# A recurrent mixer on one core: 64-row products alternate between row halves, and four stages of it are staged anew

## Chip, core and metric

One core of a Trainium2 chip runs one program with two model blocks, one after the other. The metric is device time in microseconds (us), the median over runs. The program uses TensorE (PE) for matrix products and transposes, VectorE (DVE) and ScalarE (ACT) for elementwise work, GpSimd (POOL) for little, and SyncE (SP) for issuing weight transfers.

## The reference

The change touches one function only, the recurrent mixer of the second block's last layer, on S = 256 tokens, width D = 1024 and 16 heads of N = 64:

```python
def rwkv7_mixer(h, ...):
    xx = jnp.pad(h, ((0, 0), (1, 0), (0, 0)))[:, :-1] - h
    xr, xw, xk, xv, xa, xg = [h + xx * mu[i] for i in range(6)]
    r = xr @ w_r; k = xk @ w_k; v = xv @ w_v
    w_log = -softplus(-(w0 + tanh(xw @ w_dec1) @ w_dec2)) - 0.5
    a = sigmoid(a0 + (xa @ w_a1) @ w_a2)
    g = sigmoid(xg @ w_g1) @ w_g2
    kk = l2norm_per_head(k * k_k)
    k = k * (1.0 + (a - 1.0) * k_a)
    decay = exp(-exp(w_log))
    def step(state, ...):                       # per head, 64 x 64
        sa = state @ (-kk_t)
        state = state * w_t + sa * (kk_t * a_t) + v_t * k_t
        return state, state @ r_t
    y = per_head_norm(scan(step)) * lnx_g + lnx_b
    bonus = sum(r * k * r_k) * v
    return ((y + bonus) * g) @ w_o
```

## The kernel before, in words

Function `rwkv` computes this in float32. Features lie on the partitions, 128 at a time in KC = 8 chunks of 256 tokens; a chunk holds two heads, the upper one on partitions 0 to 63 and the lower one on 64 to 127. A product of 128 rows uses all partitions, a product of one head uses a row half of 64. A float32 product is two instructions on TensorE in the trace; where operands are split into a high and a low part of type fp32r, a product is three instructions of half the passes (`mm3`, lines 180 to 182), and the splitting costs ScalarE (L168, L275) and VectorE (L169, L276) an instruction each per piece.

The stages, with their places in microseconds from the start of the profiled span:

- **Stage A, 1938.4 to 2027.1.** Low-rank products `lora` (L1597) on the mixes `xw` and `xa`; the second half of k (`lin_raw`, L1585); the head lengths (`lengths`, L1685 to L1700); the low-rank pair's second factors, decay and a, with 64 rows each (`second`, L1614, first all of decay, then g's first factor, then all of a); the running sum L (L1653) and its exponentials Pi, Pv (L1665, L1666); r from raw float32 weights; `sources` and `kappa` (L1707 to L1718), which build the scaled keys be, ka and AR; the blocks `alpha` (L1838, 64 rows each, evacuated by L1844), from which `cut` (L1860) copies the diagonal 32 x 32 blocks; `rho` (L1723, L1724); the bonus (L1791, L1792).
- **The inverse, 2027.1 to 2058.4.** `invert32` runs 62 small steps on VectorE (L296 to L304) in a chain. TensorE meanwhile makes v (L1768), and ScalarE evacuates each half of it with 16 instructions per 128 tokens (L1754, L1756).
- **Stage B, 2058.4 to 2143.1.** The steps `inverse` for four pairs of (group of 4 heads, chunk of 128 tokens), with the rest as filler: blocks rho (L1838, masked on VectorE by L1842), `tokmajor` (L1804), `gates` (L1783); then `inverse` for the other four with `finish` of groups 0 and 1. `finish` is, for each of two token chunks tb: `pair_blocks` (L1820, 64 rows, 256 columns, masked by L1822), R (L1960 in the first chunk; L1967 with 128 rows and L1968 with 64 rows in the second), U (L1976), the state S0, and the output (L1995 and L1996; L2004 to L2006). Then come the head norm on VectorE (L2011 to L2014) and a transpose and split.
- **Stage C, 2143.1 to 2155.3**, the norm of groups 0 and 1; **stage D, 2155.3 to 2191.2**, `finish` of groups 2 and 3 with the first products of w_o. After that w_o goes on.

Work is written as generators. `weave(chains, filler, n)` takes a step from each chain and n from the filler after each; `part(gen, n)` takes n steps. The framework then orders each engine's instructions by the place in that text and by what is ready in its own model, so the order on an engine is fixed before the run. Waits between engines are semaphores. Small products go to banks of PSUM from a ring (`bank1`), and a bank is free again when its evacuation is done. `wraw` issues a weight transfer of 1 MB on SP's queue into a ring of buffers.

## Time and profile before

| | us |
|---|---|
| runs of the kernel before | 2420.02, 2418.22, 2420.16 (median 2420.02) |
| profiled execution | 2412.75, of it the span 2411.0 |
| PE busy in the span | 2350.1 (97%) |
| DVE, ACT, POOL busy | 1547.2 (64%), 1139.9 (47%), 90.2 (4%) |
| mean granted PE clock | 0.986 of full speed |

The profiled execution stands 0.3% under the median of the runs. "Busy" says that an engine has an instruction in flight, not that it is at its peak. A TensorE instruction's own duration is longer than the distance to the next one, because they are pipelined; where an instruction's cost is wanted, the distance between starts is what counts. The granted clock tells how much of TensorE's full rate was allowed in a stretch. Tile names such as ts, tp and mm are tags of PSUM banks; 64*128 in a row is rows by columns of the array used, so 64*128 is a product that uses one row half.

### The profile page before, as it was taken

The page shows a single profiled execution, that of the slowest core. Times are in us where ns is not written, and L with a number is a line of the kernel's source. Part 1 is how long each engine was busy: PE and PEld are TensorE (multiplying, and loading weights), DVE is VectorE, ACT ScalarE, POOL GpSimd, SP SyncE. Part 2 cuts the span into 40 slices and gives each one's busy share as a digit, 9 for nine tenths or more (in the row PEclk, how much of TensorE's full clock was granted, in tenths as well). Part 3 has the DMA queues.
Part 4 walks back from the last instruction along what each step waited for, and adds up shares of the span by engine and source line. Part 5 has one row for each costly group of instructions (what it writes and reads, how often), then busy time and mean ns, then how long its engine had stood idle before and what let it go on. Part 6 is the DMA issues. An engine that isn't in the chain of part 4 may idle for free.

```text
span 2411.0 us, 37594 instructions
## 1 busy us (share of the span) xinstructions
PE 2350.1 (97%) x15300; PEld 2090.5 (87%) x15300; DVE 1547.2 (64%) x2857; ACT 1139.9 (47%) x1912; POOL 90.2 (4%) x92
## 2 busy tenths in 40 slices
PE   9999999999999999999999999999999899989998
PEld 8878979899999988888799898899899776777997
DVE  6787558977788755555665576655655546536554
ACT  6556554135444444444644454544544324424443
POOL 0100002000000000000100001000000000110000
PEclk9999999999999999999999999999999989989999
DMA  4335443454444455555555542555555423102544
GB/s 175 136 123 178 158 157 123 140 177 172 160 161 172 165 195 195 195 202 192 181 178 177 211 147 98 180 178 192 184 176 191 154 79 114 53 18 97 193 175 157
DMA packets 55326, 380.15 MB, mean 158 GB/s; under 512 B 6384, under 2 KB 8048, under 8 KB 10352
## 3 DMA queue, kind: packets, MB, share of 16 engines
q1 hardware_dynamic: 55152, 377.75, 44.6%
q8 instruction: 120, 1.97, 0.3%
q14 instruction: 54, 0.44, 0.1%
HBM read 376.67 MB, written 1.05 MB: 157 GB/s over the span
## 4 chain that ended last, share of the span: by engine, by line
PE 86%; DVE 9%; ACT 2%; DMA 1%; issue 1%; POOL 1%; DVEq 0%; SPq 0%; ACTq 0%; POOLq 0%
PE acc L180 14%; PE acc L182 14%; PE acc L181 14%; PE mm L180 9%; PE mm L182 9%; PE mm L181 8%; PE mm L1585 2%; PE mm L989 2%; DVE wlo L169 1%; PE acc L1019 1%; PE mm L1575 1%; PE mm L1768 1%; ACT whi L168 0%; PE tp L245 0%; DVE H L901 0%
## 5 line engine op out<-in xcount | busy, mean ns | idle before, releaser
L169 DVE TENSOR_TENSOR wlo<-raw,whi 128x1024 fp32r<-128x1024 f32 (+1 forms) x768 | 758.2, 1000 | 450.5 <-ACT whi L168 449.1
L168 ACT ACTIVATE whi<-raw 128x1024 fp32r<-128x1024 f32 (+1 forms) x776 | 662.1, 872 | 730.9 <-PE acc L181 231.9
L180 PE MATMUL mm<-xhi,whi 128*128 128x256 f32 (+1 forms) x1368 | 395.7, 290 | 0.7 <-ACT xhi L250 0.6
L182 PE MATMUL mm<-xhi,wlo 128*128 128x256 f32 (+1 forms) x1368 | 388.6, 284 | 2.0 <-DVE wlo L169 2.0
L181 PE MATMUL mm<-xlo,whi 128*128 128x256 f32 (+1 forms) x1368 | 388.1, 284 | 0.0
L180 PE MATMUL acc<-xhi,whi 128*128 128x256 f32 x1280 | 362.5, 283 | 0.0
L182 PE MATMUL acc<-xhi,wlo 128*128 128x256 f32 x1280 | 362.2, 283 | 0.0
L181 PE MATMUL acc<-xlo,whi 128*128 128x256 f32 x1280 | 362.2, 283 | 0.0
L182 PEld LDWEIGHTS mm<-xhi,wlo 128*128 128x128 f32 (+1 forms) x1368 | 261.8, 191 | 4.1 <-DVE wlo L169 3.3
L180 PEld LDWEIGHTS mm<-xhi,whi 128*128 128x128 f32 (+1 forms) x1368 | 261.6, 191 | 3.6 <-issue 1.7
L181 PEld LDWEIGHTS mm<-xlo,whi 128*128 128x128 f32 (+1 forms) x1368 | 262.1, 192 | 0.6 <-DVE xlo L251 0.2
L181 PEld LDWEIGHTS acc<-xlo,whi 128*128 128x128 f32 x1280 | 245.7, 192 | 0.2
L180 PEld LDWEIGHTS acc<-xhi,whi 128*128 128x128 f32 x1280 | 245.7, 192 | 0.2
L182 PEld LDWEIGHTS acc<-xhi,wlo 128*128 128x128 f32 x1280 | 245.7, 192 | 0.0
L180 PE MATMUL acc<-whi,acts 128*128 128x512 f32 x424 | 164.9, 389 | 0.0
L181 PE MATMUL acc<-wlo,acts 128*128 128x512 f32 x424 | 164.9, 389 | 0.0
L182 PE MATMUL acc<-whi,acts 128*128 128x512 f32 x424 | 164.9, 389 | 0.0
L180 PE MATMUL acc<-whi,fhi 128*128 128x512 f32 x272 | 106.2, 391 | 0.1
L182 PE MATMUL acc<-whi,flo 128*128 128x512 f32 x272 | 105.9, 389 | 0.0
L181 PE MATMUL acc<-wlo,fhi 128*128 128x512 f32 x272 | 105.9, 389 | 0.0
L181 PEld LDWEIGHTS acc<-wlo,acts 128*128 128x128 f32 x424 | 79.6, 188 | 16.7
L182 PEld LDWEIGHTS acc<-whi,acts 128*128 128x128 f32 x424 | 79.6, 188 | 16.5
(767 smaller groups left out, 3817.2 us busy)
## 6 DMA issues: line engine op xcount, KB each, us to landing
raw<-in_l_ffn_gf_dram SPq DMA_DIRECT2D x80, 1024.0 KB, 4.8
raw<-in_peer_u_dram SPq DMA_DIRECT2D x64, 1024.0 KB, 4.9
raw<-in_peer_v_dram SPq DMA_DIRECT2D x64, 1024.0 KB, 4.9
raw<-in_l_ffn_wd_dram SPq DMA_DIRECT2D x44, 1024.0 KB, 4.7
raw<-in_w_gate_dram SPq DMA_DIRECT2D x8, 1024.0 KB, 4.9
raw<-in_w_pq_dram SPq DMA_DIRECT2D x8, 1024.0 KB, 4.9
raw<-in_l_ffn_gu_dram SPq DMA_DIRECT2D x8, 1024.0 KB, 4.8
raw<-in_w_mix_out_dram SPq DMA_DIRECT2D x4, 1024.0 KB, 4.9
```

Source lines behind the costliest of these rows:

```text
L168: nc.scalar.activation(out=hi[:, c:c + step], in_=raw[:, o + c:o + c + step], func=AF.Copy)
L169: eng.tensor_sub(lo[:, c:c + step], raw[:, o + c:o + c + step], hi[:, c:c + step].bitcast(F32))
L180: mm(out, lhsT=l[0], rhs=r[0], start=start, stop=False)
L181: mm(out, lhsT=l[0], rhs=r[1], start=False, stop=False)
L182: mm(out, lhsT=l[1], rhs=r[0], start=False, stop=stop)
L989: mm(o, lhsT=get[:, c:c + P], rhs=xn[:, kc, :], start=kc == 0, stop=kc == 7)
L1019: mm(ps[:, (k + i) * P:(k + i + 1) * P], lhsT=o[:, i // 2, 0, :, i % 2], rhs=z[:, i // 2, :, i % 2], start=w == 0, stop=w == 1)
L1575: mm(pk[h][:, c * P:(c + 1) * P], lhsT=kraw[c // 2][:, c % 2 * D + kc * P:][:, :P], rhs=xk(kc)[:, h * P:(h + 1) * P], start=kc == 0, stop= ...
L1585: mm(ps[:, j * S:(j + 1) * S], lhsT=raw[:, j * D + kc * P:][:, :P], rhs=x(kc), start=kc == 0, stop=kc == KC - 1)
L1768: mm(acc[h], lhsT=keep["v"](kc)[:, h * P:(h + 1) * P], rhs=raw[:, i * 512:(i + 1) * 512], start=kc == 0, stop=kc == KC - 1)
```

## The change

Five things are done in `rwkv`:

1. 64-row products of the upper and the lower row half are issued in turn, into two banks taken together; both banks are evacuated after the last product. This is done in `second`, `blocks` (alpha and rho) and `pair_blocks`. In the second chunk of `finish` two 128-row products are followed by the two 64-row products, where each 128-row product was followed by its 64-row one.
2. `second` makes decay and a in one go, and its steps stand amid k's products; L is summed in two halves (L1648).
3. r is made from split weights with `lin_feat`. The mix of r is split (L275, L276, four each) and w_r too (L168, L169, sixteen each of 128x512). The unsplit mix takes the buffer in which the squares of k were.
4. Only the first half of v fills the stretch of the inverse by the text (`part(V, 9)`); the second half follows in the second weave, and its mean is taken off on VectorE (`ev_v2`, three instructions per 128 tokens) instead of 16 on ScalarE.
5. The three GpSimd operations at the head of each `finish` (L1941 to L1943) go to VectorE (L1951 to L1953).

The diff, cut to its core:

```diff
-            def second(t, w, bias, dst):
+            def second(ts, w, biases, dsts):
 
                 for c0 in range(0, KC, 2):
-                    pb = e.bank1()
-                    for j in range(2):
-                        c = c0 + j
-                        mm(pb[:, j * S:(j + 1) * S], lhsT=w[:, c * P:(c + 1) * P], rhs=t, start=True, stop=True)
-                        nc.scalar.activation(out=dst[:, c, :], in_=pb[:, j * S:(j + 1) * S], func=AF.Sigmoid, bias=bias[:, c:c + 1])
+                    pb = [e.bank1(), e.bank1()]
+                    for c in range(c0, c0 + 2):
+                        for i in range(2):
+                            mm(pb[i][:, (c - c0) * S:(c - c0 + 1) * S], lhsT=w[i * 64:i * 64 + 64, c * P:(c + 1) * P], rhs=ts[i], start=True, stop=True)
+                    for i in range(2):
+                        for c in range(c0, c0 + 2):
+                            nc.scalar.activation(out=dsts[i][:, c, :], in_=pb[i][:, (c - c0) * S:(c - c0 + 1) * S], func=AF.Sigmoid, bias=biases[i][:, c:c + 1])
                     yield
 
...
+                sec = second((tw, ta), w2, (e.col("w0"), e.col("a0")), (ld, aT))
+                for c in hv:
+                    yield from part(sec, 2)
+
+                    nc.vector.tensor_tensor_scan(flat(L[:, c, :]), flat(sm[:, c, :]), flat(ld[:, c, :]), 0.0, OP.mult, OP.add)
                 mix(5, xg)
                 keep["tg"] = lora(xg, 1024, slice(0, P), AF.Sigmoid)
                 yield
-                yield from second(ta, w2[dn], e.col("a0"), aT)
-
-                nc.vector.tensor_tensor_scan(flat(L), flat(sm), flat(ld), 0.0, OP.mult, OP.add)
-                yield
-                keep["r"] = two_tiles(e.hip, "whi")
-                mix(0, keep["r"])
-                keep["v"] = two_tiles(e.lop, "wlo")
+                keep["r"] = [big("xm", n, F32R) for n in ("mhiB", "mhiA")]
+                xr = big("xm", "ka")
+                mix(0, chunks(xr))
+                for c in range(0, KC, 2):
+                    c = slice(c, c + 2)
+                    e.split_from(xr[:, c, :], *(t[:, c, :] for t in keep["r"]))
+                keep["v"] = chunks(big("xm", "mloA"))
                 mix(3, keep["v"])
                 yield
...
-            weave([part(p1, 1)], lk, 1)
+            weave([part(p1, 4)], lk, 1)
+            R = e.lin_feat(keep["r"], A["l1_w_r"], 8, ev_copy(rT))
             weave([prep2(), ln], R)
...
+            def ev_v2(n, h, ps):
+
+                m = vneg[:, h, n * 8:(n + 1) * 8]
+                o, i = (a.rearrange("p (h d) -> p h d", h=8) for a in (keep["vt"][:, h, n * 512:(n + 1) * 512], ps))
+                nc.vector.tensor_reduce(out=m, in_=i, axis=AX.X, op=OP.add)
+                nc.vector.tensor_scalar(out=m, in0=m, scalar1=-1.0 / 64, scalar2=None, op0=OP.mult)
+                nc.vector.tensor_tensor(out=o, in0=i, in1=m.unsqueeze(2).to_broadcast([P, 8, 64]), op=OP.add)
...
             def pair_blocks(dst, src, gr, tb):
 
                 sl = slots(gr)
+                ps = [e.bank1(), e.bank1()]
+                for s, pr, c in sl[0::2] + sl[1::2]:
+                    mm(ps[s // 2][:, (s % 2) * S:(s % 2 + 1) * S], lhsT=src[pr, c, tb * P:(tb + 1) * P],
+                       rhs=AR[pr, c, tb].rearrange("p w t -> p (w t)"), start=True, stop=True)
                 for par in range(2):
-                    ps = e.bank1()
-                    for s, pr, c in sl[par * 2:par * 2 + 2]:
-                        mm(ps[:, (s % 2) * S:(s % 2 + 1) * S], lhsT=src[pr, c, tb * P:(tb + 1) * P],
-                           rhs=AR[pr, c, tb].rearrange("p w t -> p (w t)"), start=True, stop=True)
-                    nc.vector.tensor_mul(dst[:, par * 2:par * 2 + 2, :], ps.rearrange("p (a b) -> p a b", a=2), mask)
-                    yield
+                    nc.vector.tensor_mul(dst[:, par * 2:par * 2 + 2, :], ps[par].rearrange("p (a b) -> p a b", a=2), mask)
+                yield
 
             Aa, Ar, T, TT = {}, {}, {}, {}
 
...
+                ps = [e.bank1(), e.bank1()]
+                for tb in range(2):
+                    for s, pr, c in sl[0::2] + sl[1::2]:
+                        o = (tb * 2 + s % 2) * P
+                        mm(ps[s // 2][:, o:o + P], lhsT=be[pr, c, tb * P:(tb + 1) * P], rhs=AR[pr, c, tb, w, :], start=True, stop=True)
                 for par in range(2):
-                    ps = e.bank1()
-                    for tb in range(2):
-                        for s, pr, c in sl[par * 2:par * 2 + 2]:
-                            o = (tb * 2 + s % 2) * P
-                            mm(ps[:, o:o + P], lhsT=be[pr, c, tb * P:(tb + 1) * P], rhs=AR[pr, c, tb, w, :], start=True, stop=True)
                     o = dst[gr][:, :, par * 2:par * 2 + 2, :]
-                    i = ps.rearrange("p (b s t) -> p b s t", b=2, s=2)
+                    i = ps[par].rearrange("p (b s t) -> p b s t", b=2, s=2)
                     if w:
...
-                    yield
+                yield
 
             XY = big("XY", "ra", shape=(2, 32, 32))
             X, low = XY[:, 0], XY[:, 1]
...
-                nc.gpsimd.tensor_add(w, w, lnx[:, 1, :].unsqueeze(1).to_broadcast([P, 2, 256]))
-                nc.gpsimd.tensor_mul(w, w, G)
-                nc.gpsimd.tensor_mul(G, G, lnx[:, 0, :].unsqueeze(1).to_broadcast([P, 2, 256]))
+                nc.vector.tensor_add(w, w, lnx[:, 1, :].unsqueeze(1).to_broadcast([P, 2, 256]))
+                nc.vector.tensor_mul(w, w, G)
+                nc.vector.tensor_mul(G, G, lnx[:, 0, :].unsqueeze(1).to_broadcast([P, 2, 256]))
...
                     else:
+
+                        ps = [e.bank1(), e.bank1()]
+                        o = lambda s: ps[s // 2][:, (s % 2) * P:(s % 2 + 1) * P]
+                        for ci in range(2):
+                            for s, pr, c in sl[ci::2]:
+                                mm(o(s), lhsT=KB[:, s, 0:P], rhs=vc[s % 2], start=True, stop=False)
+                            for s, pr, c in sl[ci::2]:
+                                mm(o(s)[:, pr], lhsT=AR[pr, c, 1, 0, :], rhs=S0[pr, s % 2, :], start=False, stop=True)
                         for par in range(2):
-                            ps = e.bank1()
-                            for s, pr, c in sl[par * 2:par * 2 + 2]:
-                                o = ps[:, (s % 2) * P:(s % 2 + 1) * P]
-                                mm(o, lhsT=KB[:, s, 0:P], rhs=vc[s % 2], start=True, stop=False)
-                                mm(o[:, pr], lhsT=AR[pr, c, 1, 0, :], rhs=S0[pr, s % 2, :], start=False, stop=True)
-                            nc.scalar.activation(out=R[:, :, par, :], in_=half(ps, par), func=AF.Copy, scale=-1.0)
+                            nc.scalar.activation(out=R[:, :, par, :], in_=half(ps[par], par), func=AF.Copy, scale=-1.0)
                     yield
                     U = mp.tile([P, 2, 2, 64], F32, name="U", tag="U", bufs=2)
                     Uc = [U[:, ci].rearrange("p r d -> p (r d)") for ci in range(2)]
...
             run(R, rho())
-            F = chain(bonus(), V)
+            F = chain(bonus(), part(V, 9))
             weave([invert32()], F, 1)
...
-            weave([inverse(g_, tb, Yall) for g_ in range(2, 4) for tb in range(2)] + fin[:2], iter(()), 0)
+            weave([inverse(g_, tb, Yall) for g_ in range(2, 4) for tb in range(2)] + fin[:2], V, 1)
+            run(V)
```

What that moves on the engines shows at three places. On TensorE in stage A, k's products (L1585 before, L1581 now; 32 products, 64 instructions in the trace) are followed before by the lengths (L1685) and the first of the second factors (L1614):

```order
L1597 MATMUL tp<-xm,lw 128x256 x8
L1585 MATMUL mm<-xk,raw 128x256 x32
L1685 MATMUL ts<-hk,sq 128x16 x6
L1614 MATMUL ts<-lora,w_18344 128x256 x2
L1585 MATMUL mm<-xm,raw 128x256
L1685 MATMUL ts<-hk,sq 128x16 x10
```

Now the second factors (L1610) stand in four groups of eight ahead of and between k's products:

```order
L1593 MATMUL tp<-xm,lw 128x256 x8
L1610 MATMUL ts<-lora,w_18344 128x256 x4
L1581 MATMUL mm<-xk,raw 128x256 x4
L1610 MATMUL tp<-lora,w_18344 128x256
L1610 MATMUL ts<-lora,w_18344 128x256
L1610 MATMUL tp<-lora,w_18344 128x256
L1610 MATMUL ts<-lora,w_18344 128x256
L1581 MATMUL mm<-xk,raw 128x256 x4
```

All of decay and a is issued before the last of k; x4 stands for four products, eight instructions in the trace. On TensorE in the second chunk of `finish` of group 1 (R: L1967 and L1968 before, L1978 and L1980 now):

```order
L1967 MATMUL tp<-rv,KB 128x128
L1968 MATMUL tp<-S_19459,AR 128x64
L1967 MATMUL ts<-rv,KB 128x128
L1968 MATMUL ts<-S_19459,AR 128x64
L1967 MATMUL ts<-rv,KB 128x128
L1968 MATMUL ts<-S_19459,AR 128x64
L1976 MATMUL ts<-R,TT_18990 128x128 x4
```

and now

```order
L1978 MATMUL tp<-rv,KB 128x128
L1978 MATMUL ts<-rv,KB 128x128
L1980 MATMUL tp<-S_19594,AR 128x64
L1980 MATMUL ts<-S_19594,AR 128x64
L1989 MATMUL ts<-R,TT_19121 128x128 x4
```

The 64-row products now come in twos, one of each row half, into two banks (tp, ts). On VectorE between the last steps of the inverse (L301, L302), the six operations that GpSimd did for groups 0 and 1 now stand:

```order
 L301 TENSOR_TENSOR sub<-XY,inv 128x112
+L1951 TENSOR_TENSOR ty<-ty,lnx 128x512
 L302 TENSOR_TENSOR inv<-inv,sub 128x4x28
+L1952 TENSOR_TENSOR ty<-ty,gg 128x512
 L301 TENSOR_TENSOR sub<-XY,inv 128x87
+L1953 TENSOR_TENSOR gg<-gg,lnx 128x2x256
 L302 TENSOR_TENSOR inv<-inv,sub 128x3x29
+L1951 TENSOR_TENSOR ty<-ty,lnx 128x512
 L301 TENSOR_TENSOR sub<-XY,inv 128x60
```

Four masks of rho (L1852) stand there as well, where one stood before (L1842), and TensorE's rows for the stretch of the inverse are now the first half of v (16 products), 16 blocks of rho, four transposes, the four products of `gates` and 11 products of the second half of v.

## Rows read from the trace of the kernel before

**Rows 1.** By stretch: length; PE, weight loads, DVE, ACT, POOL busy; PE clock; DMA.

```profile
1240.00:1260.00 20.00, 20.00 (x169) 20.00 (x168) 11.30 (x12) 8.89 (x11) 0.00 (x0) 1.00 0.47 162
1938.40:2027.10 88.70, 85.98 (x419) 69.20 (x419) 39.04 (x67) 39.47 (x68) 3.62 (x2) 0.92 0.28 99
2027.10:2058.40 31.30, 30.51 (x70) 13.44 (x70) 27.84 (x68) 11.99 (x64) 2.54 (x2) 0.91 0.29 101
2058.40:2143.10 84.70, 81.94 (x634) 69.64 (x632) 32.98 (x72) 37.01 (x119) 4.95 (x4) 0.94 0.10 35
2143.10:2155.30 12.20, 3.57 (x16) 2.38 (x14) 11.55 (x28) 0.87 (x2) 8.31 (x6) 0.59 0.07 21
2155.30:2191.20 35.90, 35.88 (x223) 29.47 (x223) 8.62 (x21) 6.53 (x20) 0.00 (x0) 0.90 0.00 1
```

**Rows 2.** The chain of waits in time order: start us, us, what (x pieces).

```profile
1938.59 3.46 PE ts L1597 x16
1945.50 13.81 PE mm L1585 x64
...
1994.20 7.22 DMA raw<-in_l_w_r_dram
...
2022.76 4.12 PE ts L1791 x32
...
2080.59 0.91 PE mm L1783 x2
...
2083.69 1.08 PE tp L1838 x8
```

**Rows 3.** VectorE timeline: start us, us, line, shapes, count, [idle before <-releaser].

```profile
2044.76 0.69 DVE L1842 TENSOR_TENSOR A<-ts,c_con 128x512 f32<-128x512 f32 x1 [1.24 <-PE ts L1838]
...
2051.61 1.25 DVE L301 TENSOR_TENSOR sub<-XY,inv 128x135 f32<-128x135 f32 x1
2052.89 0.30 DVE L302 TENSOR_TENSOR inv<-inv,sub 128x135 f32<-128x135 f32 x1
```

**Rows 4.** GpSimd timeline of the same stretch.

```profile
2051.42 1.27 POOL L1941 TENSOR_TENSOR ty<-ty,lnx 128x512 f32<-128x512 f32 x1 [26.32 <-ACT ty L1939]
```

**Rows 5.** TensorE timeline: 64-row mask products, one row half, then both.

```profile
2096.68 1.99 PE L1820 MATMUL ts<-AR,ka 64*128 64x256 f32 x8
...
2123.60 1.13 PE L1820 MATMUL ts<-AR,ka 64*128 64x256 f32 x8
```

**Rows 6.** TensorE timeline: a finish step of the second chunk.

```profile
2125.52 0.49 PE L1967 MATMUL ts<-rv,KB 128*128 128x128 f32 x2
2125.94 0.43 PE L1968 MATMUL ts<-S,AR 64*128 64x64 f32 x2
2126.30 0.49 PE L1967 MATMUL ts<-rv,KB 128*128 128x128 f32 x2
```

**Rows 7.** TensorE timeline: 128-row products of the first chunk.

```profile
2119.41 0.39 PE L1995 MATMUL ts<-U,A 128*128 128x128 f32 x2
2119.63 0.39 PE L1996 MATMUL ts<-rv,KB 128*128 128x128 f32 x2
```

**Rows 8.** Groups by line, 1938.4 to 2027.1: xcount, busy us, mean ns, idle before.

```profile
L1534 DVE SCALAR_TENSOR_TENSOR xm<-xx,cols,hT 128x256 f32<-128x256 f32 x22 | 8.8, 476 | 0.0
L1860 DVE TENSOR_SCALAR XY<-A 32x256 f32<-32x256 f32 x8 | 3.8, 480 | 5.2 <-ACT A L1844 5.1
L1710 DVE TENSOR_TENSOR AR<-kk,Pv 128x1016 f32<-128x1016 f32 x2 | 2.3, 1213 | 13.4 <-ACT Pv L1666 13.4
L204 DVE TENSOR_TENSOR rq_a<-rq_y 128x32 f32<-128x32 f32 x3 | 0.6, 192 | 0.1
```

**Rows 9.** Groups by line, whole span: the 512-wide weight split on VectorE.

```profile
L169 DVE TENSOR_TENSOR wlo<-raw,whi 128x512 fp32r<-128x512 f32 x330 | 224.3, 710 | 78.9 <-ACT whi L168 78.5
```

**Rows 10.** Busy time of two short stretches; columns: PE, PEld, DVE, ACT, POOL, clock, DMA.

```profile
1978.00:1992.00 14.00, 11.77 (x26) 6.88 (x27) 4.55 (x9) 5.40 (x8) 1.80 (x1) 0.63 0.00 1
2145.00:2159.00 14.00, 5.98 (x18) 4.41 (x19) 11.21 (x27) 1.19 (x2) 6.89 (x5) 0.51 0.06 19
```

More of the change, by code (lines that the diff above doesn't have):

```diff
@@ L1538, in chunks @@
                 return lambda kc: t[:, kc, :]
-            def two_tiles(pool, tag):
-                t = [pool.tile([P, 4, S], F32, name="xm", tag=tag) for _ in range(2)]
-                return lambda kc: t[kc // 4][:, kc % 4, :]
             lw = mp.tile([P, 2048], F32, name="lw", tag="AR")
@@ L1646, in prep1 @@
                 yield
-                yield from second(tw, w2[up], e.col("w0"), ld)
+                sec = second((tw, ta), w2, (e.col("w0"), e.col("a0")), (ld, aT))
+                for c in hv:
+                    yield from part(sec, 2)
+                    nc.vector.tensor_tensor_scan(flat(L[:, c, :]), flat(sm[:, c, :]), flat(ld[:, c, :]), 0.0, OP.mult, OP.add)
                 mix(5, xg)
@@ L1741, in rwkv @@
             weave([p1], ln, 1)
-            R = lin_raw(keep["r"], A["l1_w_r"], ev_copy(rT))
+            R = e.lin_feat(keep["r"], A["l1_w_r"], 8, ev_copy(rT))
             weave([prep2(), ln], R)
@@ L1770, in lin_v @@
                     for h in range(2):
-                        ev_v(n, h, acc[h])
+                        mean(n, h, acc[h])
                     yield
@@ L1778, in gates @@
                 w = wsmall("l1_w_g2")
-                g_ = gg["t"] = big("gg", "mhiA", shape=(2, D))
+                g_ = gg["t"] = big("gg", "rk", shape=(2, D))
                 for h in range(2):
@@ L2023, in rwkv @@
             run(R, rho())
-            F = chain(bonus(), V)
+            F = chain(bonus(), part(V, 9))
             weave([invert32()], F, 1)
-            TT[0], TT[1] = big("TT0", "mloB", shape=(4, 512)), big("TT1", "rk", shape=(4, 512))
+            TT[0], TT[1] = big("TT0", "mloB", shape=(4, 512)), big("TT1", "mhiA", shape=(4, 512))
             for gr in range(4):
```

20 lines of the change are left out of this document (11 added, 9 removed).

## The prediction

> **What bounds the kernel now.** I read four views in this order: busy time by stretch, the chain of waits, TensorE's and VectorE's timelines, and the groups by line. The stretches show a kernel that is bound by TensorE nearly everywhere: it is busy for 85.98 of stage A's 88.70 us, 81.94 of stage B's 84.70 and all of stage D's 35.90 [rows 1]. Two stretches differ. In the inverse VectorE runs 27.84 of 31.30 us in one chain, and in stage C TensorE has 3.57 us of work in 12.20 while VectorE is busy 11.55 [rows 1]. Two prices recur. A switch between 128 and 64 rows: a 128-row product and its 64-row one take 0.78 us from start to start (2125.52 to 2126.30), while two 128-row products stand 0.22 apart with no switch [rows 6, 7]. If the 64-row one is worth about 0.22 too, the two switches cost 0.34. And the row half: eight 64-row instructions take 1.99 us where one half works alone, and 1.13 where the other half's work lies beside them [rows 5]. The third recurring thing is the clock: it is 0.92, 0.94 and 0.90 in stages A, B, D [rows 1], and 0.63 and 0.51 in stretches with gaps on TensorE [rows 10], the lower level (1.2 GHz, 0.5 of full) after it had waited.
>
> The sum is made against the profiled execution, 2412.75 us; the runs' median is 7.3 us more, and I add that at the end.
>
> **Stage A.** Low-rank products and k start as before, 1945.5 [rows 2]. Now 32 second-factor instructions in four groups stand in k: each eight costs 1.13 [rows 5] and two switches 0.34, so 5.9 at the worst; k itself is 13.81 [rows 2]. That makes 1965.2. The 32 length products (128x16) have the form of the bonus, 4.12 [rows 2], and part of g's factor lies between them, about 1.3 of its 3.46 [rows 2]. So the lengths reach VectorE at 1970.6. The mix of r can't come earlier, because it takes the buffer that the length products read. From there VectorE runs its queue in order until the inverse: 8 mixes of r at 0.40 (8.8 over 22) 3.2 [rows 8]; 13 small steps at 0.2 2.6 [rows 8]; 4 splits of the mix and, for w_r, 12 pieces at 0.68 (224.3 over 330) 10.9 [rows 9] (of the 16 pieces four come before the lengths); 8 products kk of the mix's shape at 0.40 3.2; 14 operations of about 1024 columns at 1.17 (2.3 over 2) 16.4 [rows 8]; the cut copies 3.8 [rows 8]. That is 40.1. TensorE has less in this time: 192 split products at 0.118 (20.00 over 169) [rows 1] are 22.7, where 128 float32 ones at 0.216 (13.81 over 64) [rows 2] were 27.6; alpha and transposes beside them bring it to about 30, bonus included 34. So **VectorE, not TensorE, ends stage A**. To 40.1 I add 1.4 for the first broadcast and transpose that kk waits for, and 4.9 for the last bonus products (4.12) and their hand-over: the inverse begins at 1970.6 + 46.4 = 2017.0, against 2027.1: **-10.0**. Unknown is how long VectorE waits within its queue: nothing at best (-1.4 more), and at worst the 13.4 us that AR waited for Pv before [rows 8]. I take 1.4, since the sum L, done in two halves amid k, now comes before the lengths and not after them, and Pv with it. The transfers of w_r queue on SP behind w_g2's; a piece stood 7.22 us in the chain before [rows 2]. I cost this at nothing, because a buffer of raw weights is now free after its split and not after its products; if that cover is gone, it is the 7.2.
>
> ScalarE gets 20 splits more, at most 0.71 each by VectorE's same shape [rows 9], 14 us on 39.47 in a stage of 78: hidden.
>
> **The inverse.** VectorE's chain loses the wait of 1.24 for rho's block and gets three more masks of 0.61 to 0.69 [rows 3], +1.9; it gets six of the moved operations, of the same shape as the mask, +3.7. Before, L301 took 1.25 where the next step took 0.30, just while GpSimd's L1941 ran, and that happened twice [rows 3, 4]: -1.9. With 0.8 for waits on ScalarE's bonus rows: **+3.3**. TensorE, with the blocks of rho, gates and 11 of the second half of v moved in, has about 29 us of work in 34.6, so it idles at the end. `ev_v2` adds six operations to VectorE in stage B, some 4 us on 33 of 84.7 [rows 1]: hidden, unless a step of the inverse queues behind one (0.7, in the 5 below).
>
> **Stage B.** Removed: 2.8 of idle time (84.70 - 81.94) and 5.1 of clock (6% of 84.70) [rows 1]; gates, 8 instructions at 0.455 (0.91 over 2) 3.6 [rows 2]; rho, seven eights at 1.08 [rows 2], of which four stay at the price of both halves with switches, 4.3 net; tokmajor 0.4. Added: five products (ten instructions) of v's second half 4.5; about 5 for the low clock that the idle end of the inverse leaves, and for evacuations no longer hidden. Row halves in `finish` of two groups: four mask blocks, each 0.65 less (between 0 where they lay side by side already and 0.86, the whole 1.99 - 1.13 [rows 5]; nearer to the latter, since they were issued half by half), 2.6; R and output, eight twos, each one switch pair less and the two 64-row products side by side, 0.34 + 0.22 = 0.56 [rows 6, 7], 4.5. Sum: -2.8 - 5.1 - 3.6 - 4.3 - 0.4 + 4.5 + 5 - 2.6 - 4.5 = **-13.8**.
>
> The TensorE page of the Trainium skill speaks against the 0.22: "TensorE: Matmul & The Clock Gate", Part 3, lists weight loads as what overlaps between row groups and says that matmuls start and end in strict order. Read so, only the saved switches and weight loads would be left, and the sum would be the first rival's; the 1.13 against 1.99 [rows 5] says otherwise for this kernel.
>
> **Stages C and D.** C is VectorE's. GpSimd's six operations there [rows 1] cost VectorE at most 0.95 each (1.25 - 0.30 [rows 3]), 5.7; I take 4.6, since not each meets a small step. Six moved operations lengthen it by 3.7. D: row halves as in B, 7.1; clock, half of the missing 10% of 35.90 [rows 1], 1.7; +2.5 for evacuations after both halves instead of one during the other. Sum **-7.2**. The bounds of C are 0 and -4.6, those of D -1.5 and -11.
>
> Sum: -10.0 + 3.3 - 13.8 - 7.2 = -27.7, so 2385.0 as a profiled execution, **2392 us** in the measure of the median. Below 0.2%, 4.8 us, a measurement of this kernel can't tell a difference.
>
> **Rivals.** *No overlap of halves.* The two 64-row products run one after the other, because the second waits for a bank or for order. The row halves then give only switches (0.34 of each 0.56) and nothing on mask blocks: of 14.2 in B and D 5.4 are left; rho and the second factors lose some 3 more. About -16: 2404. For it: eight instructions at 1.99 stand in the trace too [rows 5]. Against it: both halves come from two banks taken together. Chance 0.15.
>
> *VectorE's queue waits.* In stage A a late Pv holds all behind it, w_r's splits too, by up to 13.4 [rows 8]. The inverse begins at 2029, no earlier than before; the other stages keep their gain: -27.7 + 12 = -16, 2404, or 2408 if TensorE starts the inverse at the low clock. For it: the queue is in order, and it is the bound. Chance 0.13.
>
> *The other side.* Two banks are handed over at once, so each step of `finish` and `inverse` leaves TensorE a gap of an evacuation (0.69 [rows 3]) twice over, and the gaps hold the clock down. This is priced by the stretch 1978 to 1992, where TensorE was idle for 2.2 of 14.0 us and ran at 0.63 [rows 10]: the some 66 + 27 us of work that B and D keep would take 93 / 0.63 and 15% of gaps, about 170, where the forecast has 100. That is 2462 if every step does so; from four tenths of it the gain of 27.7 is eaten, and half of it, 2427, is the price I set. [...] Against it: two chains alternate in D, and it was busy without gaps [rows 1]. Chance 0.05.
>
> **The numbers.** Forecast 0.67 (2380 to 2400), no overlap 0.15, VectorE 0.13, slower 0.05. The range 2374 to 2409 holds the forecast with the bounds of C and D, no overlap and most of the third. Faster by over 0.2% 0.91, within 0.2% 0.04, slower 0.05.
>
> **What would show it.** Right: the inverse's first transpose on VectorE near 2017, its length 34 to 35 us; L1829 (masks) 16 instructions in 2.0 to 2.3 us; L1978 with L1980 about 1.0 us per two heads; L180 to L182 of r 0.12 apart; GpSimd silent. Wrong: starts of the 64-row twos 0.22 apart; idle time on VectorE in stage A above 10 us; stages B and D at a clock under 0.85.

## The result, and the profile after

| | before | after |
|---|---|---|
| median of the runs | 2419.61 (4 runs) | 2382.89 (4 runs) |
| profiled execution, of it the span | 2412.75, 2411.0 | 2382.24, 2380.4 |
| mean granted PE clock | 0.986 | 0.988 |

The ratio of the medians is 0.9849 (95% interval 0.9832 to 0.9866): **36.7 us less**, where 27.7 less was forecast. The profiled execution of before stood 7 us under its median, so the spans differ by 30.6 only. The mixer's first product starts at 1938.43 in the trace of before and 2.4 later, at 1940.81, in that of after, with the same code ahead of it, and what follows stage D takes 1.6 longer; so the mixer's stages differ by more than the spans do. Over all traces of this study that start lies between 1938.3 and 1941.5, so from here on stages tell where time went, and the medians how much.

The page of after, its span and its busy times:

```profile
span 2380.4 us, 37698 instructions
PE 2316.9 (97%) x15364; PEld 2070.9 (87%) x15364; DVE 1557.5 (65%) x2896; ACT 1140.4 (48%) x1882; POOL 74.5 (3%) x80
```

Busy time of after by stage (stage A, the inverse, stages B, C and D; columns as in [rows 1]):

```profile
1940.80:2018.90 78.10, 72.14 (x484) 63.95 (x483) 48.78 (x89) 47.03 (x86) 3.61 (x2) 0.95 0.32 112
2018.90:2051.10 32.20, 30.52 (x98) 13.68 (x96) 30.35 (x76) 14.13 (x68) 0.00 (x0) 0.97 0.24 77
2051.10:2118.50 67.40, 65.08 (x607) 56.78 (x606) 33.02 (x78) 27.85 (x68) 0.00 (x0) 1.00 0.15 54
2118.50:2130.00 11.50, 3.01 (x11) 2.13 (x11) 9.96 (x34) 1.19 (x2) 0.00 (x0) 0.57 0.09 26
2130.00:2159.80 29.80, 29.80 (x223) 24.99 (x222) 8.13 (x23) 6.26 (x21) 0.00 (x0) 0.88 0.00 1
```

Beside [rows 1]: in stage A TensorE is busy for 72.14 of 78.10 us, where it was for 85.98 of 88.70: its idle time there grew from 2.7 to 6.0. Stage B, cut as in [rows 1], is 18 us shorter (84.70 to 66.48), and TensorE's work in it fell by as much (81.94 to 64.17) while its clock rose from 0.94 to 1.00. GpSimd is silent after stage A.

For comparisons over many kernels the stages are cut at fixed instructions (first low-rank product; L296, the inverse's first transpose; end of L304; the second, then the fourth sum of a head norm; for C the second split of its output). By these marks, in us:

| stage | before | after | difference | forecast |
|---|---|---|---|---|
| A | 88.70 | 78.10 | -10.6 | -10.0 |
| inverse | 31.24 | 32.14 | +0.9 | +3.3 |
| B | 86.34 | 67.46 | -18.9 | -13.8 |
| C | 13.78 | 11.44 | -2.3 | C and D |
| D | 33.44 | 29.83 | -3.6 | -7.2 |
| sum | 253.50 | 218.97 | -34.5 | -27.7 |

The forecast cut B, C and D elsewhere, by up to 3.2 us: at TensorE's last product of group 1's output, its first of w_o, and the last product of the output. By these cuts B fell from 84.70 to 66.48, 18.2 less, and C and D together from 48.16 to 41.36, 6.8 less.

TensorE's timeline of after, in the second chunk of `finish` of group 1 (answers to [rows 6]):

```profile
2107.99 0.49 PE L1978 MATMUL tp<-rv,KB 128*128 128x128 f32 x2
2108.32 0.39 PE L1978 MATMUL ts<-rv,KB 128*128 128x128 f32 x2
2108.63 0.32 PE L1980 MATMUL tp<-S,AR 64*128 64x64 f32 x1
2108.64 0.32 PE L1980 MATMUL ts<-S,AR 64*128 64x64 f32 x1
2108.79 0.27 PE L1980 MATMUL tp<-S,AR 64*128 64x64 f32 x1
2108.80 0.27 PE L1980 MATMUL ts<-S,AR 64*128 64x64 f32 x1
2109.00 0.49 PE L1978 MATMUL tp<-rv,KB 128*128 128x128 f32 x2
```

The 64-row instructions of the two halves (tp, ts) start 0.01 us apart. Two heads take 1.01 us (2107.99 to 2109.00), where they took 2 x 0.78 = 1.56 before [rows 6]: 0.55 less, the forecast's 0.56.

VectorE's timeline of after, near the end of the inverse (answers to [rows 3]):

```profile
2043.72 0.30 DVE L302 TENSOR_TENSOR inv<-inv,sub 128x135 f32<-128x135 f32 x1
2044.06 0.28 DVE L301 TENSOR_TENSOR sub<-XY,inv 128x112 f32<-128x112 f32 x1
2044.25 0.69 DVE L1951 TENSOR_TENSOR ty<-ty,lnx 128x512 f32<-128x512 f32 x1
2044.85 0.27 DVE L302 TENSOR_TENSOR inv<-inv,sub 128x112 f32<-128x112 f32 x1
2045.04 0.68 DVE L1952 TENSOR_TENSOR ty<-ty,gg 128x512 f32<-128x512 f32 x1
```

L302 follows L301 after 0.79 us with a moved operation between them, and a step followed the last after 0.34 without one (2043.72 to 2044.06). So the operation costs the chain 0.45 and not its 0.69: it starts 0.19 after L301, in time in which the dependent L302 would have waited anyway.

### The profile page after: what moved, and what is told of

It is laid out like the page before. It is cut to its first block, busy times and chain, and to the rows that moved or that the text cites. A ratio compares the mean times of both kernels' runs of the same rounds, so it can differ in the third digit from the quotient of the medians.

```text
span 2380.4 us, 37698 instructions
## 1 busy us (share of the span) xinstructions
PE 2316.9 (97%) x15364; PEld 2070.9 (87%) x15364; DVE 1557.5 (65%) x2896; ACT 1140.4 (48%) x1882; POOL 74.5 (3%) x80
## 4 chain that ended last, share of the span: by engine, by line
PE 83%; DVE 11%; ACT 2%; DMA 2%; issue 1%; POOL 1%; SPq 0%; DVEq 0%; ACTq 0%; POOLq 0%
PE acc L180 14%; PE acc L182 14%; PE acc L181 14%; PE mm L180 9%; PE mm L182 9%; PE mm L181 9%; DVE wlo L169 2%; PE mm L989 2%; PE acc L1019 1%; PE mm L1571 1%; DMA raw<-in_l_ffn_gu_dram 1%; PE mm L1581 1%; ACT whi L168 1%; DVE sub L301 1%; PE tp L245 0%
## 5 line engine op out<-in xcount | busy, mean ns | idle before, releaser
L169 DVE TENSOR_TENSOR wlo<-raw,whi 128x1024 fp32r<-128x1024 f32 (+1 forms) x784 | 768.0, 994 | 457.6 <-ACT whi L168 456.1
L168 ACT ACTIVATE whi<-raw 128x1024 fp32r<-128x1024 f32 (+1 forms) x792 | 671.1, 867 | 745.3 <-PE acc L181 226.5
```

The costliest lines, as they stand in the source:

```text
L168: nc.scalar.activation(out=hi[:, c:c + step], in_=raw[:, o + c:o + c + step], func=AF.Copy)
L169: eng.tensor_sub(lo[:, c:c + step], raw[:, o + c:o + c + step], hi[:, c:c + step].bitcast(F32))
```

## The experiments

Twelve kernels ran, each beside the kernel before on the same chip; the medians of before were 2418.7, 2419.3 and 2420.7 us. "The change" is 2382.9. A ratio's interval is about 4 us to either side, so a smaller difference between two kernels is told by a stage of the trace or not at all. A stage of one trace has a spread too: D, which e3, e4, e5, e7 and e9 leave as it is, takes 29.9 to 31.2 us in them and 29.83 in the change.

### Row halves: issue in turn, banks, and the finish steps

**e1_halves_in_sequence** takes both banks as the change does, but issues all of one half, then all of the other, in `second`, `pair_blocks` and `blocks`:

```diff
-                    for c in range(c0, c0 + 2):
-                        for i in range(2):
+                    for i in range(2):
+                        for c in range(c0, c0 + 2):
...
-                for s, pr, c in sl[0::2] + sl[1::2]:
+                for s, pr, c in sl:
...
-                for tb in range(2):
-                    for s, pr, c in sl[0::2] + sl[1::2]:
+                for tb, (s, pr, c) in [(tb, x) for q in (sl[:2], sl[2:]) for tb in range(2) for x in q]:
```

> The changed kernel with one thing undone: in the second factors, the blocks of alpha and rho and the mask blocks, the products of the upper row half are all issued before those of the lower; the two banks and their evacuations stay as changed. Theory (the gain of the row halves is that both halves work side by side): eight mask blocks x 0.86, the four groups of second factors x 0.86, and two of rho's eights, about 11 us slower than the changed kernel, near 2394. Rival (the gain is the saved switches alone, or is hidden behind waits): no difference, 2383.

Measured: 2385.5 us, ratio 0.9863 (0.9848 to 0.9878), 2.6 above the change. The theory of an issue that must alternate fell. TensorE's timeline of e1, second factors of decay and a in stage A:

```profile
1949.74 0.48 PE L1610 MATMUL tp<-lora,w 64*128 64x256 f32 x1
1949.75 0.48 PE L1610 MATMUL ts<-lora,w 64*128 64x256 f32 x1
1950.06 0.38 PE L1610 MATMUL tp<-lora,w 64*128 64x256 f32 x1
1950.07 0.38 PE L1610 MATMUL ts<-lora,w 64*128 64x256 f32 x1
...
1950.81 1.99 PE L1581 MATMUL mm<-xk,raw 128*128 128x256 f32 x8
```

The instruction stream of e1 has four instructions of tp, then four of ts; the trace starts them in pairs, and the eight take 1.07 us (1949.74 to 1950.81), as in the change (1951.34 to 1952.40, 1.06). TensorE found the other half's products by itself, four instructions further on. Where a half is eight instructions long it found less: the blocks of rho in the inverse take 2.82 us for 32 instructions in e1 (L1846), 2.06 in the change (L1847), and those of alpha in stage A, from start to start, 6.5 against 4.8.

**e11_banks_one_by_one** takes one bank, fills it, evacuates it and yields, as before, in `pair_blocks` and `blocks` (alpha, rho):

```diff
-                ps = [e.bank1(), e.bank1()]
-                for s, pr, c in sl[0::2] + sl[1::2]:
...
                 for par in range(2):
+                    ps = e.bank1()
+                    for s, pr, c in sl[par * 2:par * 2 + 2]:
...
-                yield
+                    yield
```

> The changed kernel with the mask blocks and the blocks of alpha and rho as before: one bank is taken, filled by one row half and evacuated, then the next. Theory (a half can run beside the other only if its bank is in hand when the other's products are issued): some of the eight mask blocks and of rho's blocks run half after half again, 5 to 8 us slower than the changed kernel, 2388 to 2391. Rival (the run with the halves in sequence moved only 2.6 us: TensorE finds the other half's products by itself): at most 2 us, 2383 to 2385.

Measured: 2397.6 us, ratio 0.9913 (0.9898 to 0.9928): 14.7 above the change, more than either theory had. Stage B alone is 14.8 longer (82.26 where the change has 67.46). TensorE's timeline of e11 there:

```profile
2096.40 1.99 PE L1830 MATMUL ts<-AR,ka 64*128 64x256 f32 x8
2098.32 1.10 PE L1904 MATMUL tp<-Y,TT 128*128 128x64 f32 x8
```

Its row by stretch:

```profile
2050.09:2132.35 82.26, 81.15 (x643) 68.61 (x641) 37.65 (x85) 28.93 (x68) 0.00 (x0) 0.96 0.14 49
```

A mask block of one group and chunk takes 1.92 us alone (2096.40 to 2098.32), where the change has two of them in that time (16 instructions of L1829, 2103.69 to 2105.61). And more of rho ends up in stage B. The group of it in the change:

```profile
L1847 PE MATMUL ts<-AR,be 64*128 64x128 f32 x32 | 2.3, 285 | 0.0
```

The groups of it in e11:

```profile
L1848 PE MATMUL ts<-AR,be 64*128 64x128 f32 x32 | 4.6, 285 | 0.0
L1848 PE MATMUL tp<-AR,be 64*128 64x128 f32 x24 | 3.5, 285 | 0.0
```

With a bank per step there are twice as many steps to weave, so 56 instructions of rho, 8.1 us, stand in B instead of 32 with 2.3. They stand in eights between 128-row transposes, and each eight pays its switches. From start to start, 3.3 us of the 14.8 are the mask blocks, 5.4 rho and 3.0 products of v that stood in the inverse; the rest lies in the neighbours. So e11 measures the two banks and the order that comes with them together, and the share of each was not run apart. What is shown is that a mask block's halves run one after the other with one bank at a time and side by side with two, while e1 shows that their alternation is not needed.

**e2_finish_as_before** sets R and the output of the second chunk of `finish` back to one 64-row product behind each 128-row one:

```diff
-                        ps = [e.bank1(), e.bank1()]
-                        for ci in range(2):
-                            for s, pr, c in sl[ci::2]:
-                                mm(o(s), lhsT=KB[:, s, 0:P], rhs=vc[s % 2], start=True, stop=False)
-                            for s, pr, c in sl[ci::2]:
-                                mm(o(s)[:, pr], lhsT=AR[pr, c, 1, 0, :], rhs=S0[pr, s % 2, :], start=False, stop=True)
                         for par in range(2):
+                            ps = e.bank1()
+                            for s, pr, c in sl[par * 2:par * 2 + 2]:
+                                mm(o, lhsT=KB[:, s, 0:P], rhs=vc[s % 2], start=True, stop=False)
+                                mm(o[:, pr], lhsT=AR[pr, c, 1, 0, :], rhs=S0[pr, s % 2, :], start=False, stop=True)
```

> The changed kernel with the second chunk of finish as before: each 128-row product is followed by its 64-row one, and each bank is evacuated as soon as it is full. Theory: 16 twos at 1.56 instead of 1.01 us, 9 us slower than the changed kernel, near 2392. Rival (earlier evacuations give back what the switches cost): at most 3 us, 2383 to 2386.

Measured: 2396.0 us, ratio 0.9905 (0.9892 to 0.9919): 13.1 above the change, where the theory had 9; stage B is 4.0 longer, D 8.2. Stage D of e2:

```profile
2133.94:2171.97 38.03, 38.03 (x222) 31.50 (x221) 8.24 (x22) 6.65 (x21) 0.00 (x0) 0.78 0.00 1
```

About the same instructions as in the change (222 and 223), TensorE without a gap in both, 8.2 us more. At the clock of the change, 0.88, it would be about 34 (38.03 x 0.78 / 0.88), an estimate; so some 4 are the switches and the two products one after the other, and some 4 the clock. That B alone, at 1.00 in both, lost 4.0, agrees with the former.

**e8_halves_alone** puts the halves of `blocks`, `pair_blocks` and `finish` on the kernel before and nothing else (a diff against before):

```diff
+                ps = [e.bank1(), e.bank1()]
+                for s, pr, c in sl[0::2] + sl[1::2]:
+                    mm(ps[s // 2][:, (s % 2) * S:(s % 2 + 1) * S], lhsT=src[pr, c, tb * P:(tb + 1) * P],
...
+                    for s, pr, c in sl[0::2] + sl[1::2]:
...
+                            for s, pr, c in sl[ci::2]:
```

> The kernel before with one part of the change: the blocks of alpha and rho, the mask blocks and the second chunk of finish in alternating row halves with both banks taken together. All else (second factors, r, v, GpSimd) as before. Theory (this part carries most of the gain; undone alone, its two pieces cost 14.7 and 13.1 us): 24 to 28 us faster than the kernel before, 2391 to 2395. Rival (the parts only pay together, because the stage bound by VectorE or GpSimd takes the gain back): 10 to 15 us faster, 2404 to 2409.

Measured: 2396.9 us, ratio 0.9905 (0.989 to 0.992): 23.8 below its own kernel before, two thirds of the whole gain and just short of the theory's 24 to 28. Stage A is 87.90 (0.8 less than before), B 72.76 (13.6 less), D 26.64 (6.8 less), while C, with GpSimd in it, is 15.64 (1.9 more).

### Stage A: r, and the place of the low-rank pair

**e3_r_raw** makes r from raw float32 weights, as before, with the rest of the change:

```diff
-                keep["r"] = [big("xm", n, F32R) for n in ("mhiB", "mhiA")]
-                xr = big("xm", "ka")
-                mix(0, chunks(xr))
-                for c in range(0, KC, 2):
-                    c = slice(c, c + 2)
-                    e.split_from(xr[:, c, :], *(t[:, c, :] for t in keep["r"]))
+                keep["r"] = chunks(big("xm", "mhiB"))
+                mix(0, keep["r"])
...
-            R = e.lin_feat(keep["r"], A["l1_w_r"], 8, ev_copy(rT))
+            R = lin_raw(keep["r"], A["l1_w_r"], ev_copy(rT))
```

> The changed kernel with r from raw float32 weights again (128 instructions of 0.216 us instead of 192 of 0.118, no splits on ScalarE and VectorE, and the mix of r waits for nothing). Theory (VectorE ends stage A): VectorE has 10.9 us less to do there, TensorE 5 more, and TensorE's work of some 39 us ends the stage: within 3 us of the changed kernel either way, 2380 to 2386. Rival (TensorE ends stage A in the changed kernel too): 5 us slower, 2388.

Measured: 2377.6 us, ratio 0.9828 (0.9815 to 0.9842): **5.3 below the change**, which neither theory had. The intervals of the two just overlap; what makes it plain is stage A, 73.84 in place of 78.10, and e12 below, where it comes again. Splitting r is a loss here. Busy time of that stage in e3:

```profile
1938.77:2012.61 73.84, 73.61 (x420) 62.49 (x419) 37.71 (x69) 34.92 (x65) 3.61 (x2) 0.98 0.33 119
```

Groups of the change in stage A, on VectorE and then on TensorE (columns as in [rows 8]):

```profile
L169 DVE TENSOR_TENSOR wlo<-raw,whi 128x512 fp32r<-128x512 f32 x16 | 10.1, 684 | 5.2 <-ACT whi L168 5.2
...
L276 DVE TENSOR_TENSOR xm<-xm 128x512 fp32r<-128x512 f32 x4 | 2.8, 698 | 0.0
L1701 DVE SCALAR_TENSOR_TENSOR kk<-rk,cols,ts 128x256 f32<-128x256 f32 x6 | 2.5, 476 | 4.4 <-PE ts L1698 4.4
...
L1711 DVE TENSOR_TENSOR AR<-kk,Pv 128x1016 f32<-128x1016 f32 x2 | 2.4, 1212 | 0.0
...
L180 PE MATMUL mm<-xm,whi 128*128 128x256 f32 x64 | 19.8, 309 | 3.0 <-ACT whi L168 3.0
L181 PE MATMUL mm<-xm,whi 128*128 128x256 f32 x64 | 19.6, 306 | 2.5 <-DVE xm L276 2.5
```

Busy time of the change in two stretches behind TensorE's two waits:

```profile
1976.80:1982.00 5.20, 5.13 (x31) 5.13 (x32) 2.24 (x8) 5.17 (x7) 0.00 (x0) 0.68 0.00 0
1989.00:1994.00 5.00, 4.77 (x26) 4.57 (x26) 5.00 (x7) 4.71 (x12) 0.00 (x0) 0.66 0.01 3
```

In e3 TensorE is busy for all but 0.23 us of the stage. In the change it waits 3.0 us for a weight's high part and 2.5 for the low part of the mix; the splits give VectorE and ScalarE 11.1 and 12.1 us more to do in the stage than in e3 (48.78 against 37.71, 47.03 against 34.92). In the 5 us behind each of the two waits the clock is 0.68 and 0.66. So the cheaper products saved almost nothing: from start to start r's 192 split instructions take 27.6 us in the change and the 128 raw ones 28.2 in e3, while TensorE's idle time is 5.7 us longer. The split saved work on TensorE at a place where the splitting engines made it wait. Which of these two weighed more was not run apart.

Why, then, is stage A of e3 14.9 us shorter than that of before? Three groups of before on TensorE in stage A:

```profile
L1585 PE MATMUL mm<-xm,raw 128*128 128x256 f32 x128 | 35.0, 428 | 0.5 <-DMA raw<-in_l_w_r_dram 0.5
...
L1614 PE MATMUL ts<-lora,w 64*128 64x256 f32 x24 | 9.4, 500 | 0.0
...
L1614 PE MATMUL tp<-lora,w 64*128 64x256 f32 x8 | 2.6, 404 | 2.2 <-DVE kk L1700 2.2
```

Its timeline, from the wait on:

```profile
1980.84 0.67 PE L1614 MATMUL tp<-lora,w 64*128 64x256 f32 x2 [2.23 <-DVE kk L1700]
1981.43 1.22 PE L1585 MATMUL mm<-xm,raw 128*128 128x256 f32 x2
1982.58 1.22 PE L1614 MATMUL ts<-lora,w 64*128 64x256 f32 x2
...
1986.03 4.63 PE L1585 MATMUL mm<-xm,raw 128*128 128x256 f32 x10
1990.59 1.22 PE L1614 MATMUL ts<-lora,w 64*128 64x256 f32 x2
```

The second factors stood one or two products at a time between those of r and others, and one of them waited 2.23 us for kk. In the stretch behind that wait the clock is 0.63 [rows 10]: a product of r takes 0.91 us there (ten instructions in 4.56, 1986.03 to 1990.59), 1.15 where it alternates with a second factor (1981.43 to 1982.58), and 0.44 at the full clock (8.83 for 40 instructions of L1581 in the change, two of them a product). The durations in the groups run past the next instruction's start. Summed over the traces from start to start, waits apart, the second factors take 10.9 us in before and 4.8 in e3, where they are four groups of eight, and r's 128 instructions 34.1 and 28.2; TensorE's idle time is 2.7 and 0.2. The three differences are 14.5 of the 14.9; the blocks of alpha give 2.4 more, and k, the bonus and the start of v take 2.3 back.

**e7_second_after_k** issues the low-rank pair after k and not amid it:

```diff
-            weave([part(p1, 4)], lk, 1)
+            weave([part(p1, 1)], lk, 1)
```

> The changed kernel with only the first step of the low-rank work amid k, as before: the second factors of decay and a, still in alternating halves, come after k and among the length products. Theory (decay early makes L, Pi and Pv early, so that VectorE's queue doesn't wait for them): Pv comes later by about 14 us, VectorE waits for it as before, stage A 5 to 10 us longer, 2388 to 2393. Rival (the place of the second factors is no matter, their work is the same): no difference, 2383.

Measured: 2381.8 us, ratio 0.9843 (0.983 to 0.9857): no difference that can be told, stage A 77.64. That it stands amid k is worth nothing. What stays as the source of the second factors' 6.1 is that both run in pairs, out of the way of r; these two were not run apart.

### The end without GpSimd, and v

**e6_gpsimd_back** gives the three operations at the head of each `finish` back to GpSimd (all three lines as this one):

```diff
-                nc.vector.tensor_mul(w, w, G)
+                nc.gpsimd.tensor_mul(w, w, G)
```

> The changed kernel with the twelve operations at the head of finish back on GpSimd. Theory (they slow VectorE's small steps when they run beside them): VectorE loses six operations of 0.5 in the inverse and six of 0.6 in stage C, and gains two slowed steps of 0.95 in the inverse and about 4.6 in C: no difference, 2382 to 2384. Rival one (sharing is the larger cost): 5 us slower, 2388. Rival two (the moved operations are the larger cost): 5 us faster, 2378.

Measured: 2389.4 us, ratio 0.9882 (0.9867 to 0.9897): 6.5 above the change. "No difference" fell, and rival one, that the sharing of the two engines is the larger cost, came close. VectorE's timeline of e6 in the inverse:

```profile
2041.47 0.28 DVE L301 TENSOR_TENSOR sub<-XY,inv 128x112 f32<-128x112 f32 x1
2041.78 1.23 DVE L302 TENSOR_TENSOR inv<-inv,sub 128x112 f32<-128x112 f32 x1
2043.04 1.28 DVE L301 TENSOR_TENSOR sub<-XY,inv 128x87 f32<-128x87 f32 x1
2044.36 1.31 DVE L302 TENSOR_TENSOR inv<-inv,sub 128x87 f32<-128x87 f32 x1
```

GpSimd's timeline of the same stretch:

```profile
2041.51 1.37 POOL L1951 TENSOR_TENSOR ty<-ty,lnx 128x512 f32<-128x512 f32 x1 [30.91 <-ACT ty L1949]
2042.96 1.27 POOL L1952 TENSOR_TENSOR ty<-ty,gg 128x512 f32<-128x512 f32 x1
2044.30 1.27 POOL L1953 TENSOR_TENSOR gg<-gg,lnx 128x512 f32<-128x512 f32 x1
```

While GpSimd works, each of VectorE's steps takes as long as GpSimd's, about 1.27 us, where it took 0.18 to 0.27 in the change. Six GpSimd operations stretch six steps by about 1.0 each; on VectorE itself the six cost some 0.45 to 0.5 each. In e6 the inverse is 3.2 longer than in the change, stage C 3.7 and B 3.0 (this last part was not followed further). Together that is more than the 6.5 of the medians; in these traces e6's mixer starts 2.5 earlier, and what follows D is 1.1 shorter. The Trainium skill, "SBUF — State Buffer", section "SBUF: two separate sides", says that VectorE with two operands in SBUF and GpSimd share a pair of ports that one of them holds for a whole instruction while the other blocks. The rows agree: 1.23 to 1.31 beside 1.27.

**e9_prep_later** and **e10_prep_after_norms** move those three operations of groups 2 and 3 out of stage C's chain. In e9 by their place in the text:

```diff
+                if gr < 2:
+                    prep()
...
+                    if gr >= 2 and tb == 0:
+                        prep()
```

> The changed kernel with the six moved operations of groups 2 and 3 put behind the first masks of these groups on VectorE, so that they don't stand among the head norms of groups 0 and 1. Theory (stage C is VectorE's chain and they lengthen it): stage C shorter by 3.0 to 3.7, near 2379.5. Rival (they fill gaps that the chain has anyway): no difference, 2383.

Measured: 2382.5 us, ratio 0.9853 (0.9838 to 0.9868). The framework put them where they had stood, so e9 only repeats the change; its stages agree with it to within 0.1 us. In e10 a dependence on the last addition of group 1's norm holds them back:

```diff
+                    x = (nc.vector.tensor_mul if n else nc.vector.tensor_add)(o, o, i)
+                    if gr >= 2:
+                        tc.add_manual_dep(x.ins, o_["pin"].ins.name, ...
...
-                nc.vector.tensor_add(y, y, w)
+                o_["pin"] = nc.vector.tensor_add(y, y, w)
```

> The changed kernel with the six moved operations of groups 2 and 3 tied behind the norm of groups 0 and 1, so that none of them stands among its small steps on VectorE. Theory (stage C is VectorE's chain, and each of the six adds its 0.6 us to it): stage C shorter by 3.0 to 3.7 us, near 2379.5. Rival (what is taken out of stage C comes back ahead of the masks of groups 2 and 3, which stand behind the six now): no difference, 2382 to 2384.

Measured: 2381.2 us, ratio 0.9841 (0.9827 to 0.9854): 1.7 below the change, within the uncertainty. Stage C falls from 11.44 to 9.49, and D rises from 29.83 to 32.03: the operations now stand between the splits and the masks with which D begins, and what C gained is given back there. How is not shown: TensorE has no gap in D in either kernel, but five instructions more and a clock of 0.85 in e10 (228 in 32.03 us; 223 at 0.88 in the change).

**e4_v_as_before** (all of v as filler of the inverse, its mean by ScalarE) and **e5_mean_scalar** (the second half's mean by ScalarE alone):

```diff
-                    mean = ev_v if n == 0 else ev_v2
+                    mean = ev_v
...
-            F = chain(bonus(), part(V, 9))
+            F = chain(bonus(), V)
```

The first line is all of e5; e4 has both, and the second weave without v.

> The changed kernel with all of v placed as the filler of the inverse again, and both halves' means taken off on ScalarE. Theory (v's second half late, with its mean on VectorE, takes away the wait of TensorE for ScalarE at the start of stage B and the low clock after it): TensorE waits 2 to 3 us and runs some 5 us at the low clock, 6 to 8 us slower than the changed kernel, 2389 to 2391. Rival (v is the same work wherever it stands): no difference, 2383.

> The changed kernel with only the mean of v's second half back on ScalarE (16 instructions per 128 tokens instead of three on VectorE). Theory (the place of v matters, and the mean too, because ScalarE's 6.5 us of small instructions stand ahead of the evacuations of the inverse): 3 to 5 us slower than the changed kernel, 2386 to 2388. Rival (only the place matters): no difference, 2383.

Measured: e4 2383.5 us, ratio 0.9848 (0.9835 to 0.9862); e5 2382.2, ratio 0.9843 (0.9829 to 0.9856). Neither can be told from the change. In e4 the inverse is 2.9 shorter and B 5.6 longer. The waits and the lower clock that its theory named are there (in B TensorE idles 3.4 us at a clock of 0.95, in the change 2.3 at 1.00), but the medians differ by 0.6 only. Both theories that gave these parts a price fell.

**e12_raw_r_and_prep_after** joins the edits of e3 and e10 (their two diffs together).

> The changed kernel with r from raw weights and the six operations of groups 2 and 3 behind the norms of groups 0 and 1, the two edits that gained 5.3 and 1.7 us alone. Theory (they act in stages A and C, which don't overlap): both gains add up, near 2376. Rival (the second was run-to-run spread): 2377.5, as with raw r alone.

Measured: 2376.6 us, ratio 0.9819 (0.9805 to 0.9832), the fastest of all, 6.3 below the change. Nearly all of that is e3's; the 1.0 below e3 is not to be told from nothing.

## Why the prediction was right, and where its steps were not

The forecast case held, faster and within the range; 9 us of the gain were missing from the sum. For the row halves the mechanism held and the price was low: 14.2 in B and D and some 3 elsewhere were forecast, and e8, which has them without the second factors, gains 23.8. In stage A the number held and the step behind it did not.

- **Stage A, -10.0 against -10.6.** From the lengths to the inverse the forecast had 40.1 us of work for VectorE and 6.3 of waits, 46.4, and 34 of work for TensorE. Busy time of after in that stretch:

```profile
1972.09:2018.91 46.82, 40.86 (x316) 38.00 (x316) 36.05 (x68) 32.00 (x55) 3.61 (x2) 0.91 0.28 97
```

VectorE is busy for 36.05 us and idle for 10.8, TensorE busy for 40.86. That 46.4 and 46.8 agree is luck: "VectorE, not TensorE, ends stage A" holds only as far as the two waits of 2.5 and 3.0 us for split parts. Behind the second, from 1988.91 on, TensorE idles 0.5 us in the 30.0 to the inverse, and VectorE waits three times, for TensorE's bonus and for what ScalarE copies of TensorE's results (2.3, 2.1 and 1.5 us). The price of 0.118 for a split product held at the full clock only; on average it was 0.144. And "-10.0" was the sum of two things of opposite sign that the prediction didn't part: some -14.9 without the split of r (e3) and +4.3 from the split. The working should have asked what the stage would take without the 10.9 us of splits in VectorE's queue.
- **Inverse, +3.3 against +0.9.** The masks and the moved operations were charged at their full 0.61 to 0.69; inserted between dependent steps one costs some 0.45 to 0.5, some 1.3 less for the nine of them. The 0.8 for waits on ScalarE's bonus rows didn't come: no wait of VectorE shows in the inverse.
- **Stage B, -13.8 against -18.9, or -18.2 by the forecast's own cuts.** The term that failed is "about 5 for the low clock that the idle end of the inverse leaves, and for evacuations no longer hidden". TensorE had no idle end: it was busy for 30.52 of 32.20 us in the inverse, with v's second half behind, and B ran at 1.00. Without that term the sum is -18.8.
- **Row halves of `finish`.** For R and the output 4.5 in B and 4.5 in D was forecast (D's 7.1 has 2.6 for mask blocks in it), 9.0 in all, and 4.0 + 8.2 = 12.2 measured by e2. The 0.56 per two heads was right; about half of D's part is clock, for which D had a term of its own. D as a whole gained only 3.6 by the marks of the table. By these marks D of before is

```profile
2158.49:2191.93 33.44, 33.44 (x219) 27.73 (x218) 8.33 (x23) 6.53 (x21) 0.00 (x0) 0.94 0.00 1
```

and e2's D, without the halves, is 38.03 at 0.78. Times the clock that is 31.4 and 29.7, so by this estimate the lower clock accounts for all of the 4.6 between them. What lowered it was not run apart.
- **Stages C and D, -7.2 against -5.9, or -6.8 by the forecast's own cuts.** By those, C is 1.4 longer (12.25 to 13.68; forecast -0.9) and D 8.2 shorter (35.91 to 27.68; forecast -6.3), in part because mask blocks that followed the first products of w_o now stand ahead of them. GpSimd's removal was undersized: 6.5 in all by e6, where the forecast had +0.9 net over the inverse and C. D did not gain the 1.7 of clock: 0.90 before and 0.89 after.
- **Place of the pair and of v.** The pair amid k and the move of v had no gain of their own in the sum, except through stage B's 4.5 of products; e7, e4 and e5 show none.
- **Rivals.** *No overlap of halves* fell: instructions of the two halves start 0.01 us apart. The rule weighed there, from the Trainium skill, "TensorE: Matmul & The Clock Gate", Part 3, that matmuls start and end in strict order, doesn't hold in these traces: in e1 the fifth instruction in program order starts 0.01 us after the first. Nor did the Trainium skill speak against the 0.22, as the prediction read it: the same part has matmuls in different row groups run concurrently. *VectorE's queue waits* fell in its kind, and its size nearly came: AR doesn't wait for Pv any more (L1711, 0.0, where it was 13.4), but from the lengths on VectorE idles 10.8 us, 4.4 of them for the transposes ahead of kk (L1698). *The other side* needed gaps that hold the clock down: TensorE idles 2.3 us in all of B's 67.4, and B ran at 1.00.
- **Signs.** Those of the row halves held: 16 mask instructions in 1.92 us, 1.01 per two heads. The inverse took 32.1, not 34 to 35. And one sign of being wrong came in: VectorE idles more than 10 us in stage A, 10.8 from the lengths on.

Left open: the pairing of the second factors was not run apart from the rest; its 6.1 us is read from the traces.

## What to carry to other kernels

Take both banks for the two row halves at once and evacuate behind the last product; then TensorE overlaps the halves, and for runs of four instructions a half even their order doesn't matter (e1). Before splitting float32 operands to save TensorE time, ask whether the engines that split have room ahead of it: here TensorE waited 5.5 us for split parts, ran slower behind these waits, and the cheaper product was the dearer one (e3). And work moved off GpSimd to VectorE can pay even in VectorE's own critical chain, where GpSimd stretches each of that chain's steps to its own length, and an unrelated operation fits partly between two dependent ones.

## What the runs showed of the hardware that was not expected

- Four 64-row instructions of one half issued ahead of four of the other started in pairs, eight in 1.07 us, against 1.92 with one bank after the other (e1, e11).
- An unrelated VectorE operation of 0.69 us between two dependent small ones lengthened their distance by 0.45.
- A stall of 2.23 us on TensorE in the kernel before was followed by some 10 us in which a product took 0.91 us, or 1.15 where it alternated with a 64-row one, instead of 0.44: the stretch behind it cost more than the stall.
